# Triangular solve of a hybrid diffusion step: steps over blocks of 16 rows in place of 32, with a second level of joins on TensorE

## Chip, core and metric

The kernel runs on one core of a Trainium2 chip. The core has TensorE (PE: matrix products; PEld is its weight load), VectorE (DVE), ScalarE (ACT), GpSimd (POOL) and SyncE (SP, which issues most DMAs here). Each engine runs its own queue of instructions in order, and engines wait for one another through semaphores. PE writes to PSUM, a small memory of banks that DVE and ACT read. The metric is the device time of one execution in microseconds (us), lower is better.

## What is computed

The kernel is one inference step of two layers (an even layer with latent attention beside a gated DeltaNet, an odd layer with mLSTM, each followed by a SwiGLU FFN) for 512 latent tokens and 128 context tokens. The part that matters here is the solve in the DeltaNet of the even layer. For each chunk of 64 tokens, head and direction, a strictly lower triangular 64x64 matrix plus the identity is inverted:

```python
def gated_delta_scan(q, k, v, g, beta, s0):
    ...
    a_mat = jnp.where(strict, jnp.einsum('cbhid,cbhjd->cbhij', kb, kc) * decay, 0.0)
    t_mat = lax.linalg.triangular_solve(a_mat + eye, jnp.broadcast_to(eye, a_mat.shape),
                                        left_side=True, lower=True)
    u = jnp.einsum('cbhij,cbhjv->cbhiv', t_mat, vc * bc[..., None])
    w = jnp.einsum('cbhij,cbhjd->cbhid', t_mat, kb * jnp.exp(gc)[..., None])
    ...
    s, o = lax.scan(step, s0.astype(F32), (u, w, attn, q_dec, k_dec, g_last))
```

There are 640 tokens, so 10 chunks, 8 heads and 2 directions: 160 matrices. The scan that uses them goes from chunk to chunk in order.

## The kernel before

All tokens stand side by side (`T` = 640 columns, five tiles `t` of 128 tokens, tile 4 is the context). `even_mixer` runs in stages. It loads x, norms it and splits it into two parts `hi` and `lo`. Then it makes the columns of the combined input projection one by one: `col(u)` runs 48 matmuls of 128x320 (`lin`, L369), and a few small matmuls for the modulation of later layers go before each (`ada_step`, L498, whose weights `wa` come by SP). The columns are, in order: k and q columns (`kqv_col`), five latent columns with the five calls of `chunk(t, d_)` between them, the four v columns (`kqv_col(8)` to `(11)`) and the four z columns (`gz_col`). A v column is read by ACT into `pad`, convolved on DVE (`y`, L1041), goes through a tanh on ACT and becomes `vF` on DVE (L1050); PE transposes `vF` (L1070) in the middle of a later column. PSUM holds two wide tiles `mm` and three single ones.

`chunk(t, d_)` (L1084 and on) writes the masked matrices into `Bg[g]`: group 0 holds tiles 0 and 1, group 1 tiles 2 and 3, group 2 tile 4 (half as many). A `Bg` is [128, 32, 64]: partitions are two halves `hf` of 64 rows, then 32 matrices, then 64 columns.

`solve` inverts the 32x32 blocks on the diagonal. A 32x32 transpose on DVE (L1372, L1375) turns `Bg` so that each of the 128 partitions owns one block, whose 1024 elements lie in the free dimension (`X`, and `X2` for group 2). Then 31 steps follow, two instructions each: an outer product into `tmp` (L1386) and a subtraction from `X` (L1387). Step j works on (31-j)*(j+1) elements. Groups 0 and 1 run on DVE, group 2 on POOL. A mask `low` clears what lies above the diagonal (L1395, L1396).

`solved` joins two inverted 32x32 blocks into a 64x64 inverse, group by group: DVE transposes back (`DT` L1403, `DN` L1404), PE forms `Z` (L1412, a 32x32 matmul for each matrix and half, 64 for a full group), ACT copies it with its sign changed (L1417), PE forms the corner block (L1425 for one direction, L1427 for the other, 32 each), and ACT and POOL put the result together in `TT` (L1432 to L1441), which SP writes to `scr` in HBM. `run(solved(...), expand, 1, 1)` lets one step of `solved` alternate with one of `expand` (`mla_expand`): its q part multiplies each token tile by `w_uq` (L1560 with 384 columns), norms, transposes (L1572) and stores; its kv part (L1560 with 512 columns) follows. After `solved`, the scan (L1464 and on) reads `J` from `scr` and alternates with the rest of `expand`, then with the attention heads, and before each of these a further `ada` step is taken whose weights come through the buffers `wr`. `wa`, `wr` and `J` all go through SP's queue.

The order on each engine is not that of the source: a scheduler with a timeline of its own sorts instructions when the program is built, and an engine then keeps to that order. The lines

```python
X01, X2, low, last = solve(s, vp, Bg)
with s.tc.issue_after(last.ins):
    nc.gpsimd.tensor_tensor(rq, nqk[:, 0], v3("mhalf"), op=ALU.pow)
...
run(solved(s, s.pool("ez", 1, ez), X01, X2, low, Bg, put), expand, 1, 1)
```

are where the two functions are called.

Of the kernel before, what the change touches and what calls it, by code (L numbers as in the profile page):

```python
# [10 lines left out]
ALU = mybir.AluOpType  # L11
# [4 lines left out]
P = 128  # L16
# [20 lines left out]
TT = 3  # L37
# [8 lines left out]
def _consts():  # L46
    p = np.arange(P)
# [33 lines left out]
            ("half32", (p[:, None] // 32) % 2 == np.arange(2)[None, :]),  # L81
        ],
# [11 lines left out]
    r = {}  # L94
# [22 lines left out]
def _prep(inp):  # L117
# [4 lines left out]
    d["low32"] = np.broadcast_to(np.tril(np.ones((32, 32), f)).reshape(1, 1024), (P, 1024))  # L122
# [738 lines left out]
def even_mixer(s):  # L861
# [8 lines left out]
    with ExitStack() as es:  # L870
# [97 lines left out]
        with ExitStack() as ec:  # L968
# [226 lines left out]
            kx["p"] = s.pool("ekv", 1, ec, side="right")  # L1195
# [18 lines left out]
            X01, X2, low, last = solve(s, vp, Bg)  # L1214
# [146 lines left out]
def solve(s, pool, Bg):  # L1361


    nc = s.nc
    X = s.t(pool, [P, 2, 32, 32], "X", 1)
    X2 = s.t(pool, [P, 32, 32], "X2", 1)
    tmp = s.t(pool, [P, 3, 256], "tmp", 1)
    diag = lambda x: x.rearrange("p i c -> p (i c)")[:, 0:1024:33]
    for g, eng in ((0, nc.vector), (2, nc.gpsimd), (1, nc.vector)):
        x = X2 if g == 2 else X[:, g]  # L1370
        bv = lambda j0: Bg[g][:, :, j0:j0 + 32].rearrange("p n j -> p j n")
        nc.vector.transpose(out=x, in_=bv(0))  # L1372
        for q in (1, 3):
            r = slice(32 * q, 32 * q + 32)
            nc.vector.transpose(out=x[r], in_=bv(32)[r])  # L1375
        nc.gpsimd.memset(diag(x), 1.0)
        if g == 2:

            low = Bg[2][:, 16:, :].rearrange("p n c -> p (n c)")
            nc.sync.dma_start(low, s.I["low32"])  # L1380
            low = low.rearrange("p (i c) -> p i c", i=32)
        for j in range(31):
            n, m = 31 - j, j + 1
            sh = [P, n, m]
            tv = tmp[:, g, :n * m].rearrange("p (i c) -> p i c", i=n)
            eng.tensor_tensor(tv, x[:, j, j + 1:].unsqueeze(2).to_broadcast(sh), x[:, j, :m].unsqueeze(1).to_broadcast(sh), op=ALU.mult)  # L1386
            i = eng.tensor_tensor(x[:, j + 1:, :m], x[:, j + 1:, :m], tv, op=ALU.subtract)  # L1387
        if g == 2:
            last = i
    return X, X2, low, last  # L1390


def solved(s, pool, X, X2, low, Bg, put):
    nc = s.nc
    nc.gpsimd.tensor_tensor(X2, X2, low, op=ALU.mult)  # L1395
    nc.vector.tensor_tensor(X, X, low.unsqueeze(1).to_broadcast([P, 2, 32, 32]), op=ALU.mult)  # L1396
    Rs = [X[:, 0], X[:, 1], X2]
    for g in (0, 1, 2):
        TT = s.t(pool, [P, 32, 64], "TT", 2)

        DT = s.t(pool, [P, 32, 32], "DT", 1)
        DN = s.t(pool, [P, 32, 32], "DN", 1)
        nc.vector.transpose(out=DT.rearrange("p n i -> p i n"), in_=Rs[g])  # L1403
        nc.vector.transpose(out=DN.rearrange("p n c -> p c n"), in_=Rs[g].rearrange("p i c -> p c i"))  # L1404
        ni = 16 if g == 2 else 32
        ranges = [(0, ni // 2, 0), (ni // 2, ni, 1)]
        Zp = s.mm()
# [718 lines left out]
```

## Time and profile before

| what | us |
|---|---|
| median of 3 runs (lowest, highest) | 1851.85 (1848.32, 1854.29) |
| profiled execution: its own time | 1855.94 |
| profiled execution: span from first to last instruction | 1854.1 |

| engine, whole span | busy us | share |
|---|---|---|
| PE | 1757.3 | 95% |
| PEld | 1619.3 | 87% |
| DVE | 1192.0 | 64% |
| ACT | 744.7 | 40% |
| POOL | 465.0 | 25% |

A share is a mean over stages with different limits. Lines of the trace have the start in us from the span's start, the duration, the engine, the line of the source, the operation, out<-in with sizes, and a count where neighbours are merged; in brackets stands the idle time of that engine before it and what ended it. A plain fp32 matmul leaves two MATMUL records. PEclk is the granted clock of TensorE as a share of 2.4 GHz; the other level is 1.2 GHz.

### The profile page before, as it was taken

The numbers are of one execution on the slowest core, as the hardware profiler recorded it, in microseconds if no ns is written. First come the engines' busy times: TensorE is split into PE (matmuls) and PEld (weight loads), VectorE is DVE, ScalarE is ACT, GpSimd is POOL, SyncE is SP. The second block draws the span as 40 slices with busy tenths as digits, with TensorE's granted clock in tenths as the row PEclk, the third lists the DMA queues.
The fourth block names the chain that finished last, engine by engine and source line by source line (L and its number), as shares of the span: only waits on it lengthen the run. The fifth ranks groups of instructions, "written<-read, shape, count | busy, mean of one in ns | idle before, by whom it ended". The sixth has DMA issues, their size and how long they took to land.

```text
span 1854.1 us, 33865 instructions
## 1 busy us (share of the span) xinstructions
PE 1757.3 (95%) x13775; PEld 1619.3 (87%) x13775; DVE 1192.0 (64%) x2191; ACT 744.7 (40%) x1474; POOL 465.0 (25%) x424
## 2 busy tenths in 40 slices
PE   6998788889999989999999999999998999999999
PEld 3887678665668989999999999898998999999999
DVE  5578998665674688448637573544657873684473
ACT  3453225522345455325415343620336551453251
POOL 2024583311110154024214000021304331340230
PEclk9998888889999989999999999998999999999999
DMA  9565543696642212322322334421321233223222
GB/s 367 161 202 176 174 134 96 177 276 200 191 139 92 69 52 86 94 65 83 101 69 75 112 102 124 132 73 42 114 69 46 80 92 92 69 81 92 68 72 89
DMA packets 99327, 214.40 MB, mean 116 GB/s; under 512 B 8060, under 2 KB 44604, under 8 KB 97764
## 3 DMA queue, kind: packets, MB, share of 16 engines
q1 hardware_dynamic: 94548, 206.14, 35.9%
q10 hardware_dynamic: 4624, 6.11, 1.2%
q8 instruction: 108, 1.77, 0.4%
q14 instruction: 47, 0.39, 0.1%
HBM read 190.68 MB, written 21.54 MB: 114 GB/s over the span
## 4 chain that ended last, share of the span: by engine, by line
PE 76%; DVE 9%; DMA 6%; ACT 3%; POOL 3%; issue 2%; SPq 1%; ACTq 0%; DVEq 0%; POOLq 0%
PE mm L369 29%; PE p L350 18%; PE mm L350 12%; PE pa L498 2%; DMA wr<-in_w_ada 2%; PE p L1734 1%; PE p L1757 1%; PE p L1997 1%; PE p L1744 1%; PE p L2001 1%; SPq L1893 1%; ACT hf L787 1%; DMA D<-grd 1%; PE p L399 1%; PE p L1530 1%
## 5 line engine op out<-in xcount | busy, mean ns | idle before, releaser
L284 ACT CAST wp<-wr 128x1024 fp32r<-128x1024 f32 (+2 forms) x224 | 187.9, 839 | 502.3 <-PE mm L369 360.2
L369 PE MATMUL mm<-hi,wp 128*128 128x320 f32 x1696 | 336.3, 316 | 1.1 <-DVE x L542 0.7
L285 DVE TENSOR_TENSOR wp<-wr,wp 128x1024 fp32r<-128x1024 f32 (+2 forms) x220 | 255.9, 1165 | 75.8 <-ACT wp L284 68.6
L369 PEld LDWEIGHTS mm<-hi,wp 128*128 128x128 f32 x1696 | 271.5, 191 | 14.6 <-issue 9.9
L369 PE MATMUL mm<-hf,wp 128*128 128x320 f32 x1836 | 279.8, 311 | 0.6 <-DVE x L542 0.4
L369 PEld LDWEIGHTS mm<-hf,wp 128*128 128x128 f32 x1836 | 274.0, 189 | 1.1 <-PE mm L369 1.1
L369 PE MATMUL mm<-lo,wp 128*128 128x320 f32 x848 | 199.1, 315 | 0.2 <-DVE lo L454 0.2
L542 DVE SCALAR_TENSOR_TENSOR x<-mm,ada,x 128x320 f32<-128x320 f32 (+2 forms) x174 | 66.1, 434 | 201.5 <-PE mm L369 191.6
L350 PE MATMUL p<-T,wp 128*128 128x320 f32 x1164 | 185.4, 308 | 0.0
L350 PEld LDWEIGHTS p<-T,wp 128*128 128x128 f32 x1164 | 174.4, 188 | 0.0
L285 DVE TENSOR_TENSOR wp<-st,wp 128x512 fp32r<-128x512 f32 x160 | 137.5, 881 | 23.1 <-ACT wp L284 21.6
L369 PEld LDWEIGHTS mm<-lo,wp 128*128 128x128 f32 x848 | 144.8, 191 | 1.6 <-DVE lo L454 0.5
L350 PE MATMUL p<-B,wp 128*128 128x320 f32 x864 | 143.2, 309 | 0.0
L310 POOL TENSOR_TENSOR st<-st,wr 128x512 f32<-128x512 f32 x40 | 53.4, 1336 | 346.4 <-DMA wr<-in_w_fi 122.8
L284 ACT CAST wp<-st 128x512 fp32r<-128x512 f32 x160 | 95.9, 621 | 101.9 <-PE p L350 43.6
L350 PEld LDWEIGHTS p<-B,wp 128*128 128x128 f32 x864 | 130.9, 188 | 0.0
L350 PE MATMUL mm<-T,wp 128*128 128x320 f32 x756 | 120.0, 309 | 0.0
L350 PEld LDWEIGHTS mm<-T,wp 128*128 128x128 f32 x756 | 113.1, 188 | 0.0
L350 PE MATMUL mm<-B,wp 128*128 128x320 f32 x576 | 95.0, 309 | 0.0
L350 PEld LDWEIGHTS mm<-B,wp 128*128 128x128 f32 x576 | 87.1, 188 | 0.0
L621 POOL TENSOR_TENSOR a<-a,p 128x320 f32<-128x320 f32 x40 | 36.8, 920 | 146.0 <-DVE p L582 141.6
L310 POOL TENSOR_TENSOR st<-wr,st 128x512 f32<-128x512 f32 x40 | 69.8, 1745 | 7.6 <-DVE wp L285 7.6
(495 smaller groups left out, 2905.1 us busy)
## 6 DMA issues: line engine op xcount, KB each, us to landing
wr<-in_w_fi SPq DMA_DIRECT2D x68, 512.0 KB, 3.6
wa<-in_w_ada SPq DMA_DIRECT2D x52, 512.0 KB, 7.1
wr<-in_w_ada SPq DMA_DIRECT2D x44, 512.0 KB, 6.1
wr<-in_w_fo SPq DMA_DIRECT2D x32, 512.0 KB, 3.5
wr<-in_w_odd SPq DMA_DIRECT2D x25, 512.0 KB, 3.8
wr<-in_w_even SPq DMA_DIRECT2D x22, 512.0 KB, 4.5
J<-scr SPq DMA_DIRECT2D x20, 512.0 KB, 7.4
w<-in_w_fi SPq DMA_DIRECT2D x20, 512.0 KB, 3.6
```

Source lines behind the costliest of these rows:

```text
L284: s.nc.scalar.copy(hi, raw)
L285: (eng or s.nc.vector).tensor_tensor(lo, raw, hi.bitcast(F32), op=ALU.subtract)
L310: eng.tensor_tensor(whole[f], x, y, op=op)
L350: s.nc.tensor.matmul(out, a[:, k, :], op(k, n, p), start=(k == 0 and q == 0 and not onto), stop=(k == nk - 1 and q == 2), skip_group_check ...
L369: s.nc.tensor.matmul(ps[:, n, :320], a[:, k, :], op(k, n, p), start=(k == 0 and q == 0), stop=(k == nk - 1 and q == 2))
L399: s.nc.tensor.matmul(o, a[:, k, :], op(k, n, p), start=(k == 0 and q == 0), stop=(k == nk - 1 and q == 2))
L498: nc.tensor.matmul(ps[32 * g:32 * g + 32, :256], s.cs[:, k, :], w[:, g * 256:(g + 1) * 256], start=(k == 0), stop=(k == KD - 1))
L542: s.nc.vector.scalar_tensor_tensor(x[:, a:b], in0=ps[:, a - 320 * n:b - 320 * n], scalar=gate[:, k, i:i + 1], in1=x[:, a:b], op0=ALU.mult, ...
L621: nc.gpsimd.tensor_tensor(a1, a1, p5, op=ALU.mult)
L787: nc.scalar.activation(b_[:, r], t[:, r], AF.Identity, bias=s.sh[:, o, i:i + 1], scale=s.sw[:, o, i:i + 1])
L1530: nc.tensor.matmul(vp[hf][rows, a, b], J[rows, 0, c0:c0 + 64], vn[rows, c0:c0 + 64], start=True, stop=True)
L1734: nc.tensor.matmul(sa, qT[:, a, t, :], kf[:, a, :512], start=True, stop=True)
```

## The change

The 32x32 blocks on the diagonal are split into two 16x16 blocks. The class `Solve` takes the place of `solve` and `solved`.

- `eliminate(g)` runs for all three groups on DVE: 15 steps of two instructions, each over both 16x16 blocks at once (2*(15-j)*(j+1) elements, 1360 in the sum over j), then a mask. ACT first collects the blocks on the diagonal in `Dg` (three copies for each group), so that one DVE transpose for each group is left in place of three. ACT and POOL then clear in `Bg` all but the blocks that the new join needs.
- `joined(g, pool)` has a new first level: PE multiplies by the block below the diagonal (`Zv`), DVE forms the identity minus that (`X`, a scalar_tensor_tensor from PSUM), PE forms the 32x32 inverse (`Tv`) and its transpose (`Nv`), ACT copies both into `DT` and `DN`. That is 128 matmuls of 32x32 three times over for a full group, on all four strips of 32 partitions, and half of it for group 2. The second level is the old `solved`.
- `eliminate` of all groups and `joined` of groups 0 and 1 are called ahead of `run`, in the source behind the z columns; only `joined(2)` still alternates with `expand`.
- The pool `ekv` is closed earlier, and `Dg` gets a pool of its own.

```diff
-            kx["p"] = s.pool("ekv", 1, ec, side="right")
+            kv = ExitStack()
+            dp = s.pool("esd", 1, ec, side="right")
+            kx["p"] = s.pool("ekv", 1, kv, side="right")
...
-            X01, X2, low, last = solve(s, vp, Bg)
+            kv.close()
+            sv = Solve(s, vp, Bg, put, dp)
+            with ExitStack() as e2:
+                zp = s.pool("ez0", 1, e2, side="right")
+                for g in range(3):
+                    last = sv.eliminate(g)
+                for g in range(2):
+                    for _ in sv.joined(g, zp):
+                        pass
...
-                run(solved(s, s.pool("ez", 1, ez), X01, X2, low, Bg, put), expand, 1, 1)
+                run(sv.joined(2, s.pool("ez", 1, ez)), expand, 1, 1)
...
+    def eliminate(s, g):
...
+        nc.scalar.copy(D[:, :ni], B[:, :ni, 0:32])
+        for r in odd:
+            nc.scalar.copy(D[r, :ni], B[r, :ni, 32:64])
...
+        nc.vector.transpose(out=x, in_=D.rearrange("p n j -> p j n"))
+        nc.gpsimd.memset(s.X[:, g, 0:1024:33], 1.0)
+        nc.gpsimd.memset(x[:, 0:16, 16:32], 0.0)
+
+        h = k.c("half16")
+        for r in even:
+            nc.scalar.mul(B[r, :ni, 0:16], B[r, :ni, 0:16], h[r])
+            nc.gpsimd.memset(B[r, :ni, 16:32], 0.0)
+        nc.scalar.mul(B[:, :ni, 32:48], B[:, :ni, 32:48], h)
+        nc.gpsimd.memset(B[:, :ni, 48:64], 0.0)
...
+        for j in range(15):
+            n, m = 15 - j, j + 1
+            sh = [P, 2, n, m]
+            tv = s.tmp[:, g, :2 * n * m].rearrange("p (b i c) -> p b i c", b=2, i=n)
...
+            nc.vector.tensor_tensor(bl[:, :, j + 1:16, :m], bl[:, :, j + 1:16, :m], tv, op=ALU.subtract)
...
+    def joined(s, g, pool, bufs=1):
...
+        nc.vector.transpose(out=DT.rearrange("p n i -> p i n"), in_=X)
+        nc.vector.transpose(out=DN.rearrange("p n c -> p c n"), in_=X.rearrange("p i c -> p c i"))
         ni = 16 if g == 2 else 32
...
+        for n in range(ni):
+            for q, r in enumerate(qs):
+                nc.tensor.matmul(Zv[r, n, :], Bg[g][r, n, 32 * (q % 2):32 * (q % 2) + 32], DT[r, n, :], start=True, stop=True)
+        yield 1
+        nc.vector.scalar_tensor_tensor(X[:, :ni], in0=Zv[:, :ni], scalar=-1.0, in1=s.one.unsqueeze(1).to_broadcast([P, ni, 32]),
+                                       op0=ALU.mult, op1=ALU.add)
+        Tv, Nv = mm(), mm()
+        for n in range(ni):
+            for r in qs:
+                nc.tensor.matmul(Tv[r, n, :], DN[r, n, :], X[r, n, :], start=True, stop=True)
+        for n in range(ni):
+            for r in qs:
+                nc.tensor.matmul(Nv[r, n, :], X[r, n, :], DN[r, n, :], start=True, stop=True)
+        nc.scalar.copy(DT[:, :ni], Tv[:, :ni])
+        nc.scalar.copy(DN[:, :ni], Nv[:, :ni])
+        yield 1
```

PE behind the last z column, before (mm<-hi is that column, L435 and L436 spread the norm of the latents, L1560 is the q part of expand):

```order
L369 MATMUL mm_2493<-hi_107,wp_2332 128x320 x2
L1560 MATMUL p_2886<-wp_2422,mhi_2860 128x384
L1560 MATMUL p_2887<-wp_2422,mhi_2860 128x384
L1560 MATMUL p_3001<-wp_2422,mhi_2860 128x384
L435 MATMUL mm_2548<-th_2546,consts 128x512
L436 MATMUL mm_2548<-th_2546,consts 128x128
L1560 MATMUL p_2886<-wp_2422,mlo_2861 128x384
```

The same place now (L1435 is Z of the new level, L1442 T, L1445 N, L1455 Z of the old level, L1467 and L1469 its corner blocks; B_101, B_102 and B_103 are groups 0, 1 and 2; L1602 is expand):

```order
L371 MATMUL mm_2496<-hi_107,wp_2335 128x320 x2
L437 MATMUL mm_2551<-th_2549,consts 128x512
L438 MATMUL mm_2551<-th_2549,consts 128x128
L1435 MATMUL mm_2705<-DT_2701,B_101 32x32 x128
L1442 MATMUL mm_2835<-X_2561,DN_2702 32x32 x128
L1445 MATMUL mm_2836<-DN_2702,X_2561 32x32 x128
L1455 MATMUL mm_3095<-DT_2701,B_101 32x32 x64
L1467 MATMUL mm_3162<-X_2561,DN_2702 32x32 x32
L1435 MATMUL mm_3244<-DT_3240,B_102 32x32 x33
L1469 MATMUL mm_3162<-DN_2702,X_2561 32x32 x32
...
L1442 MATMUL mm_3941<-X_2561,DN_3810 32x32 x40
L1602 MATMUL p_3904<-wp_2425,mhi_3878 128x384
```

On PE all matmuls of groups 0 and 1, and the first of group 2, now stand between the last z column and the first matmul of expand; none of them stands among the z columns.

DVE at that place, before (L1148 norms the latents, the transposes are those of group 0, mlo is the low part that expand multiplies):

```order
L432 TENSOR_TENSOR th_2546<-consts,rs_2403 128x640
L454 TENSOR_TENSOR mlo_2861<-xx_565,mhi_2860 128x640 x3
...
L1148 SCALAR_TENSOR_TENSOR xx_565<-xx_565,params,mm_2548 128x128
L1403 STREAM_TRANSPOSE DT_2791<-X_2557 128x32x32
L1404 STREAM_TRANSPOSE DN_2792<-X_2557 128x32x32
```

And now (the two transposes of group 0, DT_2701 and DN_2702, stand 15 rows higher up; DT_3809 and DN_3810 are those of group 2, DT_3240 and DN_3241 those of group 1):

```order
L1158 SCALAR_TENSOR_TENSOR y_2545<-y_2545,mm_2496 128x640
...
L1150 SCALAR_TENSOR_TENSOR xx_565<-xx_565,params,mm_2551 128x128
L1427 STREAM_TRANSPOSE DT_3809<-X_2561 128x32x32
L1428 STREAM_TRANSPOSE DN_3810<-X_2561 128x32x32
L1437 SCALAR_TENSOR_TENSOR X_2561<-mm_2705,B_103 128x1024
L1427 STREAM_TRANSPOSE DT_3240<-X_2561 128x32x32
L1428 STREAM_TRANSPOSE DN_3241<-X_2561 128x32x32
L1437 SCALAR_TENSOR_TENSOR X_2561<-mm_3244,B_103 128x1024
L1437 SCALAR_TENSOR_TENSOR X_2561<-mm_3813,B_103 128x512
L456 TENSOR_TENSOR mlo_3879<-xx_565,mhi_3878 128x640 x3
```

On DVE the identity-minus-Z of group 0 stands behind both transposes of group 2, and the low part that expand needs stands behind that of all three groups.

## Rows read from the trace of the kernel before

**Rows 1.** Five stretches: length, busy PE, PEld, DVE, ACT, POOL, PEclk, DMA share, GB/s.
```profile
165.60:200.60 35.00, 24.07 (x208) 20.55 (x208) 34.70 (x65) 9.79 (x17) 12.79 (x11) 0.82 0.45 143
200.60:286.70 86.10, 70.97 (x456) 62.36 (x456) 85.42 (x151) 16.64 (x29) 63.92 (x70) 0.83 0.47 147
286.70:330.30 43.60, 38.67 (x727) 35.76 (x726) 35.52 (x53) 29.18 (x48) 15.10 (x13) 0.80 0.33 103
330.30:440.00 109.70, 93.84 (x1205) 65.10 (x1203) 67.61 (x186) 40.02 (x90) 23.93 (x24) 0.89 0.79 225
440.00:600.00 160.00, 156.17 (x1714) 111.76 (x1714) 97.46 (x285) 68.61 (x207) 14.35 (x24) 0.98 0.50 148
```

**Rows 2.** Timeline of PE: its waits of over 1.8 us, 165 to 289 us.
```profile
172.43 2.27 PE L421 MATMUL p<-consts,y 128*128 128x1 f32 x10 [6.84 <-DVE y L418]
...
200.58 1.08 PE L498 MATMUL pa<-wa,cond 128*32 128x256 f32 x8 [4.11 <-DMA wa<-in_w_ada]
...
230.47 1.33 PE L1070 MATMUL p<-consts,vF 128*128 128x128 f32 x5 [7.46 <-DVE vF L1050]
...
256.40 1.33 PE L1070 MATMUL p<-consts,vF 128*128 128x128 f32 x5 [5.37 <-DVE vF L1050]
...
272.98 1.69 PE L421 MATMUL p<-consts,y 128*128 128x1 f32 x10 [1.88 <-DVE y L418]
...
286.25 0.46 PE L369 MATMUL mm<-hi,wp 128*128 128x320 f32 x2
288.60 0.79 PE L1560 MATMUL p<-wp,mhi 128*128 128x384 f32 x3 [1.89 <-ACT mhi L453]
```

**Rows 3.** Line L1386, then L1387, 140 to 300 us: DVE, POOL busy.
```profile
140.00:300.00 160.00, 27.51 (x62) 19.99 (x31) 0.86 0.48 152
...
140.00:300.00 160.00, 31.93 (x62) 20.71 (x31) 0.86 0.48 152
```

**Rows 4.** Timeline of DVE: transposes and steps of the solve, and a stalled neighbour.
```profile
155.57 2.00 DVE L1372 STREAM_TRANSPOSE X<-B 128x1024 f32<-128x1024 f32 x1
...
161.59 4.09 DVE L1375 STREAM_TRANSPOSE X<-B 32x1024 f32<-32x1024 f32 x2
...
188.17 4.07 DVE L1375 STREAM_TRANSPOSE X<-B 32x1024 f32<-32x1024 f32 x2
...
227.58 3.46 DVE L1050 SCALAR_TENSOR_TENSOR vF<-th,y 128x512 f32<-128x512 f32 x2
...
272.85 0.57 DVE L1386 TENSOR_TENSOR tmp<-X 128x112 f32<-128x112 f32 x2
273.34 0.57 DVE L1387 TENSOR_TENSOR X<-X,tmp 128x112 f32<-128x112 f32 x2
```

**Rows 5.** Timeline of PE: joins at two clocks, and a wide fp32 matmul.
```profile
305.31 1.61 PE L1412 MATMUL mm<-DT,B 32*32 32x32 f32 x89
...
307.65 1.67 PE L1427 MATMUL mm<-DN,X 32*32 32x32 f32 x58 [0.72 <-ACT TT L1438]
...
185.42 1.02 PE L435 MATMUL mm<-th,consts 128*128 128x512 f32 x2
```

**Rows 6.** Timeline of DVE and ACT: what a join waits for.
```profile
292.14 1.91 DVE L1148 SCALAR_TENSOR_TENSOR xx<-xx,params,mm 128x512 f32<-128x512 f32 x4
293.97 2.07 DVE L1403 STREAM_TRANSPOSE DT<-X 128x1024 f32<-128x1024 f32 x1
...
301.10 2.06 ACT L1417 ACTIVATE X<-mm 32x1024 f32<-32x1024 f32 x2
...
304.06 0.72 ACT L1434 ACTIVATE TT<-DT,conste 128x512 f32<-128x512 f32 x1 [0.91 <-DVE redq L1603]
...
306.45 1.15 ACT L1438 COPY TT<-mm 32x512 f32<-32x512 f32 x2
```

**Rows 7.** Timeline of PE: the kv part begins, and a wait behind it.
```profile
330.33 0.50 PE L1560 MATMUL p<-wp,mhi 128*128 128x512 f32 x1
...
355.42 0.95 PE L498 MATMUL pa<-wr,cond 128*32 128x256 f32 x6 [2.20 <-DMA wr<-in_w_ada]
```

More of the change, by code (lines that the diff above doesn't have):

```diff
@@ L81, in _consts @@
             ("half32", (p[:, None] // 32) % 2 == np.arange(2)[None, :]),
+            ("half16", (p[:, None] // 16) % 2 == 1),
         ],
@@ L1358, in softplus @@
     return z.rearrange("p (d t s) -> p d t s", d=shape[1], t=shape[2]) if len(shape) == 4 else z
[L1361 to L1376, printed above, removed]
-        if g == 2:
[L1379 to L1390, printed above, removed]
@@ L1393, in solved, with __init__, x @@
[L1393 to L1404, printed above, removed]
-        ni = 16 if g == 2 else 32
+class Solve:
+    def __init__(s, k, pool, Bg, put, dpool):
+        s.k, s.dpool, s.Bg, s.put = k, dpool, Bg, put
+        s.X = k.t(pool, [P, 3, 1056], "X", 1)
+        s.tmp = k.t(pool, [P, 3, 128], "tmp", 1)
+        low = Bg[2][:, 16:32, :].rearrange("p n c -> p (n c)")[:, :288]
+        k.nc.sync.dma_start(low, k.I["low16"])
+        s.low, s.one = low[:, :256].rearrange("p (i c) -> p i c", i=16), low[:, 256:]
+    def x(s, g):
+        return s.X[:, g, :1024].rearrange("p (i c) -> p i c", i=32)
+    def eliminate(s, g):
+        k, nc, B, x = s.k, s.k.nc, s.Bg[g], s.x(g)
+        ni = 16 if g == 2 else 32
+        odd = [slice(32, 64), slice(96, 128)]
+        even = [slice(0, 32), slice(64, 96)]
+        D = k.t(s.dpool, [P, 32, 32], "Dg", 1)
+        nc.scalar.copy(D[:, :ni], B[:, :ni, 0:32])
+        for r in odd:
+            nc.scalar.copy(D[r, :ni], B[r, :ni, 32:64])
+        if g == 2:
+            nc.gpsimd.memset(D[:, ni:], 0.0)
+        nc.vector.transpose(out=x, in_=D.rearrange("p n j -> p j n"))
[7 more added lines that the diff above has]
+        nc.gpsimd.memset(B[:, :ni, 48:64], 0.0)
+        bl = s.X[:, g].rearrange("p (b r) -> p b r", b=2)[:, :, 0:512].rearrange("p b (i c) -> p b i c", c=32)
+        for j in range(15):
+            n, m = 15 - j, j + 1
+            sh = [P, 2, n, m]
+            tv = s.tmp[:, g, :2 * n * m].rearrange("p (b i c) -> p b i c", b=2, i=n)
+            nc.vector.tensor_tensor(tv, bl[:, :, j, j + 1:16].unsqueeze(3).to_broadcast(sh), bl[:, :, j, :m].unsqueeze(2).to_broadcast(sh), op=ALU.mult)
+            nc.vector.tensor_tensor(bl[:, :, j + 1:16, :m], bl[:, :, j + 1:16, :m], tv, op=ALU.subtract)
+        return nc.vector.tensor_tensor(bl[:, :, :, 0:16], bl[:, :, :, 0:16], s.low.unsqueeze(1).to_broadcast([P, 2, 16, 16]), op=ALU.mult)
+    def joined(s, g, pool, bufs=1):
+        k, nc, Bg, X = s.k, s.k.nc, s.Bg, s.x(g)
+        TT = k.t(pool, [P, 32, 64], "TT", bufs)
+        DT = k.t(pool, [P, 32, 32], "DT", 1)
+        DN = k.t(pool, [P, 32, 32], "DN", 1)
+        nc.vector.transpose(out=DT.rearrange("p n i -> p i n"), in_=X)
+        nc.vector.transpose(out=DN.rearrange("p n c -> p c n"), in_=X.rearrange("p i c -> p c i"))
+        ni = 16 if g == 2 else 32
+        qs = [slice(32 * q, 32 * q + 32) for q in range(4)]
+        mm = lambda: k.mm().rearrange("p a (n c) -> p (a n) c", c=32)
+        Zv = mm()
+        for n in range(ni):
[14 more added lines that the diff above has]
+        yield 1
@@ L1413, in solved @@
         yield 1
-        Zs = Rs[g]
         for hf in range(2):
             r1 = slice(64 * hf, 64 * hf + 32)
-            nc.scalar.mul(Zs[r1, :ni], Zv[r1, :ni], -1.0)
-        Fp = s.mm()
+            nc.scalar.mul(X[r1, :ni], Zv[r1, :ni], -1.0)
+        Fp = k.mm()
         Fv = Fp.rearrange("p a (n c) -> p (a n) c", c=32)
@@ L1424, in solved @@
                     if d == 0:
-                        nc.tensor.matmul(Fv[64 * hf:64 * hf + 32, n, :], DN[r1, n, :], Zs[r1, n, :], start=True, stop=True)
+                        nc.tensor.matmul(Fv[64 * hf:64 * hf + 32, n, :], DN[r1, n, :], X[r1, n, :], start=True, stop=True)
                     else:
-                        nc.tensor.matmul(Fv[64 * hf + 32:64 * hf + 64, n, :], Zs[r1, n, :], DN[r1, n, :], start=True, stop=True)
+                        nc.tensor.matmul(Fv[64 * hf + 32:64 * hf + 64, n, :], X[r1, n, :], DN[r1, n, :], start=True, stop=True)
             src = DT if d == 0 else DN
             for q in range(2):
-                x, h = TT[:, n0:n1, 32 * q:32 * q + 32], s.c("half32")[:, q:q + 1]
+                x, h = TT[:, n0:n1, 32 * q:32 * q + 32], k.c("half32")[:, q:q + 1]
                 if q:
```

7 lines of the change are left out of this document (4 added, 3 removed).

## The prediction, made before the changed kernel had been run

> **What bounds the kernel now.** I began with the five stretches [rows 1]: PE is busy 70.97 of 86.10 us while the last columns are made (200.6 to 286.7, "the column phase"), 38.67 of 43.60 in the q part of expand, and 156.17 of 160 from 440 on. PE is the bound in all of them, and DVE, although busy 85.42 of 86.10 in the column phase, matters only where PE waits for it. So the second view was PE's timeline with its waits [rows 2]. Between 200 and 287 PE waits 7.46, 5.37 and 1.88 us for DVE, because `vF` and `y` stand in DVE's queue behind steps of the solve. Before that there is one wait of 6.84 us for DVE's `y` and one of 4.11 us for the DMA of `wa`. From 440 on PE is full at a clock of 0.98, so what an earlier stage gains or loses is carried to the end almost whole. I sum shifts of PE's path, and check at each place whether DVE or ACT becomes later than PE.
>
> The profiled execution took 1855.94 us, 4.09 above the median of the three runs; I sum against it and take 4 off at the end.
>
> **1. Chunk stage, 165.6 to 200.6: −8.** The `y` for which PE waits 6.84 us [rows 2] stands on DVE behind three transposes of `solve`: 2.00 and two of 4.09 together [rows 4], with a first step or two about 7 us. The change leaves one transpose for each group, and the order puts the solve's work behind this `y`. The whole wait goes. The `wa` wait (4.11) ends on a DMA that SP issues behind one that waits for DVE; DVE stands there in the two transposes of 4.07 [rows 4], which go too. I take 1 of 4.11 at least and 4 at most. 6 to 11, I take 8, low in the range, since a transfer has its own time.
>
> **2. Column phase, 86.1 now: −21.** The waits of 7.46, 5.37 and 1.88 are 14.7 us [rows 2]. In addition the granted clock is 0.83 there [rows 1]: with two levels of 1.0 and 0.5 that is 34% of 86.1 = 29 us at half clock. About 15 of these are the waits themselves; the other 14 hold work that at full clock takes 7. 86.1 − 14.7 − 7 = 64, and I take 65 for what is left of waits (64 to 72, the upper end with no gain of clock).
>
> DVE must fit below that. Of its 85.42 busy [rows 1] nearly all of the solve's 27.51 and 31.93 [rows 3] lies here (52 of 59), with 5.9 of transposes and 2.3 of masks; 25 are left. Some of these 25 are stalls (`vF` at 227.58 holds DVE for 3.46 us [rows 4]), so 25 is on the high side. New: 90 instructions of 91 elements in the mean; those of 112 elements follow each other two in 0.49 (272.85 to 273.34 [rows 4]), so at most 90 × 0.245 = 22. Three transposes of 2.0 are 6, three masks 2, and the two transposes of group 0's join (L1427, L1428) 2 × 2.07 = 4.1 [rows 6]. 25 + 22 + 6 + 2 + 4 = 59, below 65: PE bounds, if narrowly. What ACT gets (nine copies, six scalings of at most 2 us, some 12 in all) goes into 16.64 busy of 86.10, and is covered; POOL loses its 19.99 + 20.71 of the solve [rows 3]. If DVE fits badly, a `vF` comes late as now, and up to 7 of the 21 are lost.
>
> With −8 the last column ends at about 286.7 − 8 − 21 = 257.7.
>
> **3. From the last column to expand's first matmul: 1.9 now [rows 2], 46.7 then: +44.8.** This is the price. In PE's new order all joins of groups 0 and 1 stand after the last z column and before the first L1602 (expand), so expand cannot cover them. Step by step, PE's record at 16 ns: L1412's 89 records take 1.61 [rows 5], less some 0.17 for the last one's drain.
> - To X of group 0: L437/L438 1.3 (L435 takes 1.02 [rows 5]), L1150 on DVE 1.9 and then both transposes of group 2, 2 × 2.07 [rows 6], before L1437; L1437 reads 1024 elements from PSUM, twice what one L1148 reads in 1.91/4 = 0.48, so 1.0 and 0.2 for semaphores. With 0.4 of other semaphores 9. Z of group 0 (256 records, 4.1) lies beside these transposes.
> - T and N: 256 matmuls, 512 records, 8.2.
> - ACT's copy of N 1.05 (half of L1417's 2.06 [rows 6]), a mask as L1434 0.72, the two copies of −Z 2.06, semaphores 0.3: 4.1.
> - Corners: 1.0, ACT's 1.15 as L1438 [rows 6] and 0.2, then 1.0: 3.3.
> - Group 1: its second transpose 2.1, L1437 1.2, 0.2: 3.5 (its Z beside), then 8.2, 4.1 and 3.3 again.
> - Group 2's first T matmuls and `mhi`: 3.
>
> 9 + 8.2 + 4.1 + 3.3 + 3.5 + 8.2 + 4.1 + 3.3 + 3 = 46.7. The disputed size is the record. L1412 works on two strips of 32 partitions; the new level uses four, which no row shows. If four overlap as two do, a record costs 16 × 2/4 = 8 ns; if PE falls to its low clock, it is the 25 ns of L1427 after its 0.72 wait (58 records in 1.67 [rows 5]). About 1024 records lie bare, so 8 ns gives −8 and 25 ns gives +9. I take 16, the row of the same form at full clock. Term 3 is 40 to 56.
>
> The rows show two strips that write one PSUM bank at 16 ns a record, where a record of 512 columns takes up to 1.02/2 = 0.51 us, that is 32 ns for 32 columns one after another [rows 5]; so two strips do overlap. The Trainium skill, "TensorEngine Tiling (Array Packing)", section "Gotcha 1: PSUM Pressure", says that different row tiles cannot access one bank at the same time; by it this change, whose four strips share a bank, would stay at the single pace, 32 ns, and term 3 would be 16 us longer. The trace does not agree for two strips; for four no row shows it.
>
> **4. q part of expand, 41.7 now (288.6 to 330.3): −10.7.** L435/L436 are no longer in it (−1.5). The join records of groups 0 and 1 leave it: about 512 at a mean of 18.5 ns, between the 16 and 25 above, −9.5. ACT's waits between them go, 2.4 of the 4.93 us that PE idles there [rows 1]. Group 2 brings about 300 records in place of 96, +3.3 at 16 ns, and a wait more or two, +1; the clock there is 0.80 and may rise a little, −1.6. 31 (27 to 34).
>
> **5. Behind it: −4.** The kv part starts at 330.33 now [rows 7]; from 330 to 440 PE idles 109.7 − 93.84 = 15.9 us [rows 1], part of it (2.20 [rows 7]) on `wr` DMAs in SP's queue. With groups 0 and 1 in `scr` before expand begins, the scan's `J` loads can go out earlier against the kv part. I take a quarter of the idle time, −4, between −8 and +3 (J loads ahead of `wr` in SP's queue).
>
> **Sum.** −8 − 21 + 44.8 − 10.7 − 4 = +1: 1857 for a profiled execution, 1853 for the median. Two large terms cancel: the columns get rid of DVE's waits, and PE pays the same time bare at their end.
>
> **Rivals.**
> - *A, as summed:* 1853, between 1846 and 1857.
> - *B, four strips overlap:* a record of the new level costs 8 ns, −8 in term 3 and −1 in term 4, and the `wa` wait goes whole with the column phase at 64, −4: about 1839. For it: two strips overlap already. Against it: one PSUM bank for all strips, and the short bursts with ACT and DVE waits between. The rows are as above; the Trainium skill, "TensorE: Matmul & The Clock Gate", section "Measured speedup vs the span model", says that tiles on different strips add some 4 ns each; at that, term 3 would be 12 shorter. No row bears it out on four strips.
> - *C, slower, the low clock in the joins:* the chain of term 3 is matmul bursts of 2 to 8 us with waits of 3 to 5 us on ACT and DVE between. After such waits the rows show 25 ns a record (L1427), and the clock of the stretch with the joins is the lowest of the five, 0.80 [rows 1]. 1024 × 9 ns = +9 in term 3, +2 in term 4, and the first matmuls of expand begin at half clock, about +3: 1867. It decides against the old kernel once a record in term 3 costs over 21 ns (with +5 it passes 1857.4). Strips that shut each other out of the bank give the same time.
> - *D, slower, the columns don't come sooner:* DVE's 59 of 65 us leave little slack, and the order inside decides; if two of the three `vF`/`y` waits stay (7.46 and 5.37) with half clock around them, 19 of the 29 us of terms 1 and 2 are lost: 1872. Against it: DVE loses 59.44 of steps [rows 3] for 22.
>
> **How the numbers follow.** What a measurement of this kernel can tell from no change is about 0.3%, 5.6 us. A 0.38, B 0.33, C 0.19, D 0.10. A's time is the forecast, 1853; its own range ends at about the same bound (1846.3 to 1857.4), so it is "within 0.3%". B is "faster", C and D are "slower" (0.29). The range takes in B and C, with the bounds of terms 1 and 2 on B's side (−5) and D's lower half: 1834 to 1872; outside lie B with every other bound low, and the worse half of D.
>
> **What the profile of the changed kernel would show.** Term 1: no wait of 6.84 at `y` L418. Term 2: last L371 matmul of the z columns at 256 to 266, DVE waits there below 3 us in sum. Term 3: first L1602 at about 304; L1442 and L1445 at 16 ns a record (B: near 8; C: 25 and PEclk near 0.5). Term 4: the first 512-column L1602 about 31 us after the first of 384. Term 5: the distance from there to the end 4 us shorter. The forecast is wrong if the joins of groups 0 and 1 are bare for under 35 us or over 60, or if DVE still holds up the columns by more than 7.

## The result, and the profile of the changed kernel

| | before | changed |
|---|---|---|
| median, us (lowest, highest) | 1851.85 (1848.32, 1857.08) | 1870.65 (1866.34, 1877.72) |
| span of the profiled execution, us | 1854.1 | 1868.9 |

The ratio is 1.0106, 95% interval 1.0073 to 1.0140: the change costs 1% of the time. The forecast was 1853 and "no difference"; the range (1834 to 1872) holds the result, on the side to which 0.29 was given.

Six stretches of the changed kernel, to be read against [rows 1]; columns as there: length, busy PE, PEld, DVE, ACT, POOL, PEclk, DMA share, GB/s.

```profile
165.60:189.30 23.70, 21.99 (x211) 18.79 (x209) 18.98 (x34) 11.88 (x17) 12.90 (x11) 1.00 0.62 196
189.30:253.40 64.10, 61.80 (x458) 54.98 (x458) 58.36 (x140) 27.74 (x47) 15.80 (x18) 1.00 0.61 190
253.40:323.00 69.60, 41.80 (x2261) 38.39 (x2260) 15.46 (x15) 18.77 (x25) 4.80 (x6) 0.55 0.15 48
323.00:356.20 33.20, 29.26 (x455) 26.26 (x451) 19.21 (x41) 18.11 (x34) 10.78 (x9) 0.86 0.36 93
356.20:440.00 83.80, 72.45 (x898) 50.96 (x900) 56.33 (x152) 30.98 (x61) 21.63 (x18) 0.92 0.88 244
440.00:600.00 160.00, 152.83 (x1809) 100.72 (x1805) 97.55 (x298) 70.03 (x221) 16.30 (x28) 0.99 0.51 150
```

The first two rows hold the same columns as 165.6 to 286.7 before: PE is busy almost without a break, at full clock. The third row is new: 69.6 us between the last column and expand's first matmul (L1602), PE busy for 41.8 of them at a clock of 0.55. The timeline of PE at its beginning and its end (start, duration, line, count, and in brackets the idle time before and what ended it):

```profile
252.93 0.46 PE L371 MATMUL mm<-hi,wp 128*128 128x320 f32 x2
...
255.87 1.69 PE L1435 MATMUL mm<-DT,B 32*32 32x32 f32 x178 [1.40 <-DVE y L1158]
261.29 1.29 PE L1435 MATMUL mm<-DT,B 32*32 32x32 f32 x78 [3.73 <-issue]
263.91 0.95 PE L1442 MATMUL mm<-X,DN 32*32 32x32 f32 x50 [1.33 <-DVE X L1437]
265.02 1.93 PE L1442 MATMUL mm<-X,DN 32*32 32x32 f32 x128 [0.16 <-issue]
268.48 1.23 PE L1442 MATMUL mm<-X,DN 32*32 32x32 f32 x76 [1.52 <-issue]
...
271.93 1.93 PE L1445 MATMUL mm<-DN,X 32*32 32x32 f32 x128 [1.52 <-issue]
275.38 1.13 PE L1445 MATMUL mm<-DN,X 32*32 32x32 f32 x69 [1.52 <-issue]
...
322.99 1.01 PE L1602 MATMUL p<-wp,mhi 128*128 128x384 f32 x2
```

Two things are to be seen. In a piece without a hole the pitch (the time from one record's start to the next) is short. It is the duration of the piece less that of a single record, over the records that are left: 178 records in 1.69 us, (1.69 - 0.17)/177 = 8.6 ns at full clock, and later 128 in 1.93, (1.93 - 0.24)/127 = 13.3 ns at the low clock. The clock is 0.96 from 256 to 261 and 0.50 from 261.3 on: it fell during the first hole. Yet PE stops in the middle of a loop whose matmuls wait for nothing: "issue" means that the profile shows no releaser. The stops come every 128 records whatever the line is, and from one to the next it is 268.48 - 265.02 = 3.46 and 271.93 - 268.48 = 3.45 us, 27 ns a record (in group 1, from 298.78 to 302.51 and 306.51, 3.73 and 4.00). The waits of the stretch by cause (total, times, longest):

```profile
PE mm L1445 <- issue: 6.9, 4, 2.1
PE mm L1435 <- issue: 5.6, 2, 3.7
PE mm L1467 <- ACT X L1459: 3.7, 4, 1.1
PE mm L1442 <- DVE X L1437: 3.6, 3, 1.4
PE mm L1442 <- issue: 3.6, 4, 1.5
PE mm L1455 <- issue: 2.2, 2, 1.2
PE mm L1435 <- DVE y L1158: 1.4, 1, 1.4
PE mm L1469 <- ACT TT L1480: 0.9, 2, 0.4
```

18.3 of the 27.8 us of idle time are "issue". The profile has DMA queues of the kind "instruction". Between 255 and 323 the busiest of them moved (queue, kind: packets, MB, share of the DMA engines):

```profile
q8 instruction: 17, 0.28, 1.7%
```

That is a packet of 16 KB every 4 us; in the old kernel the 130 us from 200 to 330 had 9. In the two holes from 268.5 to 275.4 there are 2 packets: one for each piece of 128 records and their 128 weight loads. So the first theory of the study, **S** (supply): PE's instructions arrive in pieces of 128 records and no faster than one piece in some 3.45 us; a run of small matmuls that is longer than what is on hand goes at 27 ns a record, not at its own 8.6 or 13.3. Its rivals: **K**, the low clock is the price and the holes are incidental; **P**, strips shut one another out of a PSUM bank; **W**, the waits on ACT and DVE between the levels; **M**, the matmuls are too many wherever they stand.

### The profile page after: what moved, and what is told of

Read it like the earlier page. It is cut to its first block, busy times and chain, and to the rows that moved or that the text cites. A ratio compares the mean times of both kernels' runs of the same rounds, so it can differ in the third digit from the quotient of the medians.

```text
span 1868.9 us, 37656 instructions
## 1 busy us (share of the span) xinstructions
PE 1768.6 (95%) x15695; PEld 1629.4 (87%) x15695; DVE 1146.9 (61%) x2156; ACT 764.9 (41%) x1498; POOL 424.3 (23%) x374
## 5 line engine op out<-in xcount | busy, mean ns | idle before, releaser
L371 PE MATMUL mm<-hi,wp 128*128 128x320 f32 x1696 | 330.4, 312 | 1.1 <-DVE x L544 0.7
L371 PEld LDWEIGHTS mm<-hi,wp 128*128 128x128 f32 x1696 | 266.1, 188 | 13.3 <-issue 8.5
```

What stands on the lines that cost most here:

```text
L371: s.nc.tensor.matmul(ps[:, n, :320], a[:, k, :], op(k, n, p), start=(k == 0 and q == 0), stop=(k == nk - 1 and q == 2))
```

## Experiments

Medians of the kernel before, taken beside the runs, were 1850.8 in the first group of runs (the first four), 1853.1 (the next three), 1849.4 (two) and 1854.2 (the last two).

### 1. N issued twice

```diff
+        for n in range(ni):
+            for r in qs:
+                nc.tensor.matmul(Nv[r, n, :], X[r, n, :], DN[r, n, :], start=True, stop=True)
         for n in range(ni):
             for r in qs:
                 nc.tensor.matmul(Nv[r, n, :], X[r, n, :], DN[r, n, :], start=True, stop=True)
```

> The changed kernel with the matmuls of N issued twice over: 512 more records in the bare run of joins of groups 0 and 1, no new wait on ACT or DVE. The stretch from the end of the last column to expand's first matmul is 70.2 us in the changed kernel. Theory S (supply): 512 x 27 ns = +13.8, 84 us, nearly all of it as further holes on 'issue' or stretched pieces. Theory K (low clock, 13.5 to 14 ns a record): +7, 77 us. If neither counts (8.5 ns a record, the pitch of the first piece of 178 records): +4.4, 74.6.

One time, 1895.5 us. The stretch (last column's end at 253.97, first L1605 at 339.94) is 86.0 against 69.6 us: +16.4, 32 ns for each of the 512 added records, none of which waits for another engine. S said 13.8, K 7 (the 70.2 us of the expectations is this stretch, counted from a little earlier). The pieces here are 3.45 to 4.0 us apart, 27 to 31 ns a record. The holes stand in the added loop (L1448) as in the old one:

```profile
277.17 1.23 PE L1445 MATMUL mm<-DN,X 32*32 32x32 f32 x76 [1.80 <-issue]
...
280.62 1.93 PE L1448 MATMUL mm<-DN,X 32*32 32x32 f32 x128 [1.52 <-issue]
284.08 1.13 PE L1448 MATMUL mm<-DN,X 32*32 32x32 f32 x69 [1.52 <-issue]
```

### 2. N on DVE

```diff
-        Tv, Nv = mm(), mm()
+        Tv = mm()
...
-        for n in range(ni):
-            for r in qs:
-                nc.tensor.matmul(Nv[r, n, :], X[r, n, :], DN[r, n, :], start=True, stop=True)
         nc.scalar.copy(DT[:, :ni], Tv[:, :ni])
-        nc.scalar.copy(DN[:, :ni], Nv[:, :ni])
+        nc.vector.transpose(out=DN[:, :ni], in_=DT[:, :ni])
```

> The changed kernel with N made by a 32x32 transpose of the copied T on DVE in place of PE's 128 matmuls and ACT's copy: 512 fewer records in the bare run. DVE waits there anyway, 18 and 26 us at a time. Theory S (supply): -13.8 and about -2 for ACT's copies of N that the next step waited for, the stretch falls from 70.2 to 52 to 57 us, time 1854 to 1858. Theory K: -7 and -2, 61 us, time 1860 to 1863. Theory W (waits on ACT and DVE between the levels are what costs): -2 at most, 68 us, time 1867 to 1871.

Median 1861.0, ratio to before 1.0053 (1.0030 to 1.0076). The stretch is 56.6 us (251.66 to 308.29), 13.0 shorter, 25 ns for each record left out. S had the stretch right (52 to 57, K 61, W 68). The whole time fell by 9.7, less than S's 12 to 16, and 1861.0 is a time that K gave: the kv part starts 16.1 us earlier than in the changed kernel (340.13, 356.18), but the first matmul of the output projection comes 242.7 us behind that, 239.8 in the changed kernel, and a few us more are lost behind the projection, where the kernels are alike. The transpose of DVE is short:

```profile
269.59 1.25 DVE L1444 STREAM_TRANSPOSE DN<-DT 128x1024 f32<-128x1024 f32 x1 [7.00 <-ACT DT L1443]
```

### 3. Two banks in turn

```diff
-            for r in qs:
-                nc.tensor.matmul(Tv[r, n, :], DN[r, n, :], X[r, n, :], start=True, stop=True)
+            for q, r in enumerate(qs):
+                m = (n + ni // 2 * (q % 2)) % ni
+                nc.tensor.matmul(Tv[r, m, :], DN[r, m, :], X[r, m, :], start=True, stop=True)
```

The same for Z and N.

> The changed kernel with the order of the new level's matmuls changed so that neighbours on PE write to two PSUM banks in turn (strips 0 and 2 work half a group ahead of strips 1 and 3); the same count, the same result. Theory P (strips shut one another out of a bank): the pitch of a piece without holes falls below 8.5 ns and the stretch of 70.2 us shrinks by 5 us or more. Theories S, K and W: within 2 us of 70.2, the same pitch and the same holes.

One time, 1868.3 us; the stretch is 69.9 us (253.61 to 323.52), and the first piece reads as before:

```profile
256.09 1.69 PE L1436 MATMUL mm<-DT,B 32*32 32x32 f32 x178 [1.41 <-DVE y L1158]
261.57 1.28 PE L1436 MATMUL mm<-DT,B 32*32 32x32 f32 x78 [3.79 <-issue]
```

178 records in 1.69 us with one bank or with two: P falls. As the prediction read the rule of the Trainium skill ("TensorEngine Tiling (Array Packing)", section "Gotcha 1: PSUM Pressure"), strips that share a bank would have shown a longer pitch than strips that don't; the trace does not agree, for four strips of 32x32 fp32, each of which writes 32 partitions of its own.

### 4. Joins beside expand

```diff
-                for g in range(2):
-                    for _ in sv.joined(g, zp):
-                        pass
...
-                run(sv.joined(2, s.pool("ez", 1, ez)), expand, 1, 1)
+                zp = s.pool("ez", 1, ez)
+                run((x for g in range(3) for x in sv.joined(g, zp)), expand, 1, 1)
```

> The joins of all three groups alternate with expand, as the joins of the kernel before do; the steps over 16 rows and the new level are kept. Theory S (PE's instructions arrive too slowly for a long run of small matmuls: in the changed kernel the run of joins between the last column and expand is cut by holes of 1.2 to 3.7 us that end on 'issue', about 3.45 us from one piece of 128 records to the next, 27 ns a record): wide matmuls between the joins give the supply time, so no hole on 'issue' above 0.5 us is left in the joins, the last column still ends at 252 to 256, and the kv part starts at 311 to 323 (356 in the changed kernel, 330 in the kernel before). Some of the 11 us that the changed kernel gains behind the kv part's start is lost again. Time 1836 to 1850. Theory K (the low clock in the run of joins, 0.56, is what costs): the same direction, since the clock rises beside wide matmuls, but the holes on 'issue' stay: 1845 to 1858. Theory M (the matmuls are simply too many, wherever they stand: 42 us of busy PE): the kv part starts at about 339, time 1856 to 1864.

Median 1871.5, ratio 1.0101 (1.0073 to 1.0129): no gain at all, a miss of S as I had put it. The kv part did start early (328.43, 356.18 in the changed kernel), but the joins went on until 375.6 and the holes stayed, 22.5 us of them:

```profile
274.57 2.34 PE L1440 MATMUL mm<-X,DN 32*32 32x32 f32 x254
278.88 0.20 PE L1440 MATMUL mm<-X,DN 32*32 32x32 f32 x1 [1.98 <-issue]
...
282.34 1.93 PE L1443 MATMUL mm<-DN,X 32*32 32x32 f32 x128 [1.52 <-issue]
```

The joins of groups 0 and 1 still stand in runs of 256 to 640 records. By S, wide matmuls ahead of such a run help only by what they let be fetched in advance; here the first holes come after 151 records of Z and 254 of T. So S was put anew: not the neighbourhood but the length of a run decides. The next two runs test this form of S.

### 5. Both, and both in finer grains

The coarse kernel has the edits of 2 and 4. The fine-grained one has them too, and lets the joins give way to expand after every 32 matmuls, and expand give way inside a token tile:

```diff
         for n in range(ni):
             for r in qs:
                 nc.tensor.matmul(Tv[r, n, :], DN[r, n, :], X[r, n, :], start=True, stop=True)
+            if n % 8 == 7 and n < ni - 1:
+                yield 1
...
-        ps = tokmm(hi, lo, t, ws, 3, 384)
+        ps = yield from tokmm(hi, lo, t, ws, 3, 384)
```

Z and the old level get such yields too, and `tokmm` one after each of its `k` but the last.

> Both earlier edits together: the joins of all groups alternate with expand (as in the run with joins beside expand, 1871.5), and N is a transpose on DVE (640 records fewer on PE). In that run the pieces of joins are still 256 to 512 records long and hold 22.5 us of holes on 'issue', so standing beside wide matmuls did not help by itself. Theory S (supply of PE's instructions, 27 ns a record once a piece is longer than the 150 to 180 records that are on hand): -640 x 27 ns = -17, about 1854, holes of 6 to 12 us in all. Theory K (low clock, 13.5 ns a record): -9, 1863, holes unchanged per record.

> As the run before it, with the same instructions, but in finer grains: the joins give way to expand after every 32 matmuls (64 records) and expand gives way inside a token tile, so that most pieces of joins are 32 to 64 matmuls long between wide ones (the first two pieces stay at 128). Theory S: pieces shorter than what is on hand have no holes; 2 to 5 us of holes are left, all in the two long pieces; time 5 to 10 us below the run before, 1844 to 1850. Theory K: the count and the clock are the same, within 3 us of the run before. Theory M (the matmuls are too many in any place): within 3 us of the run before.

The coarse one: one time, 1857.6, 13.9 below the kernel of section 4 for 640 records fewer, 22 ns each (S 27, K 13.5); holes 12.1 us. The fine-grained one: median 1847.1, ratio to before **0.9970 (0.9947 to 0.9992)**, 0.3% faster than the kernel before. PE has 15055 records in both runs. The fine-grained one reads:

```profile
264.82 1.09 PE L1433 MATMUL mm<-DT,B 32*32 32x32 f32 x105 [2.04 <-issue]
...
276.25 0.22 PE L1441 MATMUL mm<-X,DN 32*32 32x32 f32 x2 [1.97 <-issue]
...
303.56 0.62 PE L1603 MATMUL p<-wp,mhi 128*128 128x512 f32 x2
304.02 0.60 PE L1617 MATMUL p<-consts,qkt 128*96 128x128 f32 x4
304.55 0.75 PE L1441 MATMUL mm<-X,DN 32*32 32x32 f32 x64
305.23 0.64 PE L1617 MATMUL p<-consts,qkt 128*96 128x128 f32 x4
305.80 0.75 PE L1441 MATMUL mm<-X,DN 32*32 32x32 f32 x64
306.48 0.73 PE L1603 MATMUL p<-wp,mhi 128*128 128x512 f32 x2
```

A piece of 64 records takes 0.75 us, (0.75 - 0.17)/63 = 9.2 ns each, with no hole. The only holes of any size, 2.04 and 1.97 us, stand in two pieces that the scheduler left at 256 records; in all 4.8 us.

How much of the 10.5 us between the two runs is due to the grain? 4.5 us are there before any join: the last column ends at 250.4 and 254.9, in code that the finer grain does not touch. From there to the output projection the fine-grained run takes 319.4 us and the coarse one 325.4: 6.0 less, for 7.3 us less of holes. So S holds in its second form, and M falls: the matmuls are the same and only their grain moved the time. K can't be told from S by this pair, since the granted clock rose too, from 0.80 (254.9 to 380) to 0.90 (250.4 to 380). K falls by sections 1 and 2, where a record cost 32 and 25 ns and K gives 13.5.

### 6. Group 0 among the z columns, and expand ahead

Two ways to cut the holes that are left. One puts the joins of group 0 between the last z columns:

```diff
+            def js(g):
+                yield from sv.joined(g, zp)
+            jj = js(0)
             for u in range(1, 4):
                 last = gz_col(u)
...
+                for _ in range(3):
+                    next(jj, None)
```

(the elimination of all groups moves ahead of the loop). The other gives expand six steps ahead of the fine-grained run:

```diff
+                for _ in range(6):
+                    next(expand)
                 run((x for g in range(3) for x in sv.joined(g, zp)), expand, 1, 1)
```

> As the fine-grained run, but the joins of group 0 really stand among the last two z columns (in pieces of 32 to 74 matmuls), those of groups 1 and 2 beside expand. Theory S: the columns end 6 to 9 us later (768 records at 8.5 ns and a wait or two), expand is 10 to 12 us shorter, next to no holes: 2 to 6 us below the fine-grained run, 1839 to 1847, faster than the kernel before. Against it (theory W): the transposes of group 0 come late on DVE and PE waits for them among the columns: 1850 or more.

> The fine-grained run (N on DVE, joins beside expand in pieces of 32 matmuls) with expand six steps ahead, so that the two pieces of 128 matmuls, which hold 4.0 us of its holes on 'issue', are cut to 8 to 64 as well. Nothing else changes, but the joins end some 5 us later, and the scan, which needs those of groups 0 and 1, begins as much later. Theory S: no hole on 'issue' above 0.5 us is left, 3 to 5 us below the fine-grained run, 1842 to 1845. Theory L (the scan's late beginning is what bounds by now): the holes go, but waits behind 340 take their place, 1846 to 1851.

Group 0 among the columns: median 1859.8, ratio 1.0035 (1.0018 to 1.0052). That is W's side (1850 or more): the columns end at 265.8, and PE waits among them and behind them (230 to 300):

```profile
PE mm L1441 <- DVE DT L1433: 5.3, 2, 3.3
PE mm L1474 <- ACT X L1466: 1.8, 2, 1.1
PE mm L1449 <- DVE X L1444: 1.5, 1, 1.5
```

Not all of it is W: from 300 to 600 PE waits 22.7 us for `wr`, 13.5 in the fine-grained run.

The second: median 1860.0, ratio 1.0044 (1.0027 to 1.0061). The holes in the joins are gone but for one of 1.2 us, and still the time is 13 us above the fine-grained run, beyond what either theory said. One wait of 4.2 us without a releaser now stands elsewhere, amid the modulation's matmuls, which are no long run of small ones; what it is stays open:

```profile
345.04 2.34 PE L500 MATMUL pa<-wr,cond 128*32 128x256 f32 x17 [4.21 <-issue]
```

The last column ends 3.6 us later than in the fine-grained run (253.9, 250.4), the scan begins at 374.5 in place of 365.3, and the output projection, which needs it, at 581.5 in place of 569.8. From the scan's first matmul to the projection's it is 204.0 us in section 4, 205.4 in the coarse run, 204.5 in the fine-grained one, 206.9 here. In these four runs the scan begins 58 to 75 us behind the kv part, and it looks as if it then set the end; that is argued from the four distances and not tested.

### 7. An earlier scan

The fine-grained run with two pieces of joins for each step of expand, and with three pieces of half the size:

```diff
-                run((x for g in range(3) for x in sv.joined(g, zp)), expand, 1, 1)
+                run((x for g in range(3) for x in sv.joined(g, zp)), expand, 2, 1)
```

> The fine-grained run (N on DVE, joins beside expand in pieces) with two pieces of joins for each step of expand in place of one. Pieces get longer, so some more holes on 'issue' come back (8 to 14 us in place of 4.8), but the joins end sooner and with them the scan's beginning: from its first matmul to the first matmul of the output projection it takes 204 to 207 us in the four runs in which it begins at 365 to 392, and 230 to 244 in those in which it begins at 338 to 355. Theory L (a scan that begins after about 350 is the bound): it begins at 330 to 345 now, the output projection at 552 to 564 (569.8 in the fine-grained run), time 1828 to 1841. If supply alone counts (theory S without L): more holes, so 3 to 8 us above the fine-grained run, 1850 to 1855.

> Between the two runs: pieces of 16 matmuls, three for each step of expand. The scan begins some 5 us later than with two pieces of 32, with fewer holes. Theory L: 1830 to 1843, within 4 us of the run with two pieces of 32. Theory S without L: 1848 to 1853.

Medians 1863.2, ratio 1.0064 (1.0042 to 1.0085), and 1862.2, 1.0054 (1.0033 to 1.0074): slower than either theory said. The scans did begin earlier (342.1 and 353.1), and yet the projection came later, at 587.1 and 583.3, 245.0 and 230.2 us behind. Theory L's threshold does not hold either: with N issued twice the scan begins at 375.5 and the projection 244.1 us behind it, and in the run of section 8 at 362.1 and 235.1 behind. What the four runs near 205 us share is that the kv part had started long before the scan, not the time at which the scan begins. PE's first cause of waits from 250 to 600 in the fine-grained run, and then in the run with two pieces:

```profile
PE pa L500 <- DMA wr<-in_w_ada: 13.5, 7, 4.0
```

```profile
PE pa L500 <- DMA wr<-in_w_ada: 23.0, 14, 4.9
PE mm L1466 <- ACT X L1458: 5.4, 4, 3.6
PE mm L1441 <- issue: 4.9, 2, 2.5
PE mm L1433 <- issue: 4.2, 2, 2.2
```

Holes of 9.1 against 4.8 us, 9.5 us more for the `wr` of the modulation steps, and 5.4 us for ACT. The run with half-size pieces, for which fewer holes had been expected, has 11.7 us of them and 21.1 us for `wr`. What sets the best place of the scan between these ends is left open; loads of `J` and `wr` in one queue are a likely reason, and were not tried apart.

### 8. Group 2's steps on POOL

```diff
+            e = nc.gpsimd if g == 2 else nc.vector
...
-            nc.vector.tensor_tensor(bl[:, :, j + 1:16, :m], bl[:, :, j + 1:16, :m], tv, op=ALU.subtract)
+            e.tensor_tensor(bl[:, :, j + 1:16, :m], bl[:, :, j + 1:16, :m], tv, op=ALU.subtract)
```

The outer product likewise.

> The changed kernel with the 15 steps of group 2 on POOL, as the 31 steps of group 2 were in the kernel before; everything else as in the changed kernel. It takes 30 steps of about 0.25 us off DVE. Theory D1 (the columns came sooner because DVE has fewer elements to go through): the last column ends within 1.5 us of the changed kernel's 253.2, or a little sooner, since DVE gets freer. Theory D2 (a good part came from DVE no longer sharing with POOL): DVE's steps and y beside POOL's steps get longer, 0.3 to 0.5 us in place of 0.2 to 0.25, PE waits again for vF or y, and the last column ends 3 us or more later. Time 1867 to 1872 by D1, 1872 to 1878 by D2.

One time, 1871.8. The last column ends at 260.8 in place of 253.4; 3.1 us of that are there before the steps begin (L437 of the earlier norm at 181.30 in place of 178.24), so 4.3 are the edit's: the column phase (from the first L500 behind `asb` to the end of the last column) takes 68.4 us, and 62.0 to 64.7 in the ten runs that keep group 2's steps on DVE and all joins behind the columns. DVE's steps beside POOL got longer, in the mean (180 to 255; busy, mean ns):

```profile
L1419 DVE TENSOR_TENSOR X<-X,tmp 128x30 f32<-128x30 f32 (+7 forms) x30 | 10.3, 361 | 0.2
L1418 DVE TENSOR_TENSOR tmp<-X 128x30 f32<-128x30 f32 (+7 forms) x30 | 9.8, 343 | 0.5 <-POOL X L1403 0.3
L1418 POOL TENSOR_TENSOR tmp<-X 128x30 f32<-128x30 f32 (+7 forms) x15 | 8.0, 533 | 0.9
```

The subtraction takes 361 ns against 323 in the changed kernel, the outer product 343 against 330, and PE waited 5.1 us for `vF` in place of 1.8. That is D2's sign, in one run; the time of the whole doesn't tell D1 from D2.

## Why the prediction was right or wrong, step by step

| term | predicted | measured | from |
|---|---|---|---|
| 1 chunk stage | -8 | -11.3 | first L498/L500 after `asb`: 200.58, now 189.30 |
| 2 column phase | -21 | -22.0 | 86.1, now 64.1 |
| 3 bare joins | +44.8 | +67.7 | 1.9, now 69.6 |
| 4 q part of expand | -10.7 | -8.5 | 41.7, now 33.2 |
| 5 behind it | -4 | -11.1 | 1523.8, now 1512.7 |
| sum of the profiled spans | +1 | +14.8 | 1854.1, now 1868.9 |

**Terms 1 and 2 were right, mechanism and size.** The waits of [rows 2] are gone (0.60 us at `y`, in sum 2.3 at `vF` and `y` among the columns), the clock went from 0.83 to 1.00, and the column phase took 64.1 us where 65 was taken. DVE was busy for 58.4, as the 59 of the check. Term 1 came out at the upper end that the text gave (11), since the 4.11 us for `wa` went as a whole.

**Term 3 is the step that failed.** Its order was right: the joins of groups 0 and 1 stand bare, and the steps came in the order written down. Its size was not: they are bare for 69.6 us, beyond the 60 that the prediction itself named as its sign of being wrong. "PE's record at 16 ns" was taken from L1412, in pieces of at most 128 records [rows 5], and no run of joins in the kernel before is longer than some 160. With four strips a record costs 8.6 ns (rival B was right on that), and at the low clock 13.3 (rival C was right that the clock falls: 0.55). But a run of 512 records goes at neither price: it took 12.6 and 13.0 us, some 25 ns a record, near the 27 ns at which its pieces of 128 come. Along the chain, where 9, 8.2, 4.1, 3.3, 3.5, 8.2, 4.1, 3.3 and 3 had been written, PE took 10.5, 12.6, 6.0, 6.0, 6.1, 13.0, 5.8, 6.0 and 3.6. Of the 22.9 us that the term lacked, 9.2 are the long runs of T and N. 4.1 are the two steps that end on the new level's Z: it was to lie beside DVE's transposes, but with its holes (3.7 and 1.8 us) it ended after them, and DVE waited 1.5 and 2.5 us for it. 3.6 are the steps with the old level's Z, which have a hole each (1.2 and 1.0), 0.6 the last step. The 5.4 of the corners have no hole: they run at the low clock, 58 records in 1.76 us, and wait for ACT. So 16.9 of the 22.9 us stand in steps with holes; the 18.3 us of holes are not to be taken off one for one, since the records of T and N between them go faster than the 16 ns of the sum.

**Term 4** was 2 us too hopeful: PE waits 3.28 us for ACT (`st`) at 349.05.

**Term 5** has two parts. From the kv part's start to the output projection 3.7 us were gained (243.5, now 239.8), as the -4 said; whether by earlier `J` loads, as it took, is not shown. The other 7.3 lie behind the projection, where the kernels are alike. In the third 320 us after it the old kernel's profiled execution had a lower clock than the new one's, and got through 40 records less, some 6 us of work (windows of before, then of after; the same columns as above):

```profile
1213.82:1533.82 320.00, 310.90 (x2098) 293.65 (x2097) 208.31 (x390) 127.05 (x231) 88.98 (x79) 0.96 0.23 74
```

```profile
1235.95:1555.95 320.00, 310.35 (x2138) 293.82 (x2137) 211.79 (x392) 128.02 (x232) 88.51 (x80) 0.99 0.23 74
```

The code of this stretch is the same, so I put this down to the two executions and not to the change. The profiled execution of before was 4.1 us above its median, and the medians differ by 18.8, the spans by 14.8.

**The rivals.** B's pitch came true and its result did not (its terms add up to 1840, not 1839); C's low clock came true, at 13.3 ns in place of 25; D did not happen. D's time, 1872, lay nearest to the result and C's, 1867, next, and neither for the reason that it gives: that the range held is luck. A fifth case was missing, and it decided: that PE could be short of instructions.

## What to carry to other kernels

When a change adds many small matmuls, price them twice: by the pitch of a short piece, and by the longest run in which they will stand, since a run longer than any in the old trace can meet a limit that no row shows. Cutting the runs into pieces between wide matmuls and taking a third of the new level off PE (a DVE transpose of 1.25 us in place of 128 matmuls) turned +1.0% into -0.3%, with the steps over 16 rows kept. And of the 30 us by which the kv part starts earlier in that run than in the kernel before (299.9, 330.3), 4 were left at the output projection (569.8, 573.8): follow a gain to the next consumer before counting it.

## What the runs showed of the hardware

- Where nothing wide stood between, PE went through long runs of small fp32 matmuls at one piece of 128 records (with their weight loads) in 3.45 to 4.0 us, with one 16 KB packet of the instruction queue a piece; a first run of 151 to 254 records went through without a hole. The records added in section 1 cost 32 ns each, those taken away in section 2 saved 25. That the packets are what PE waited for is argued from their pace; what sets that pace no run shows.
- Four strips of 32x32 fp32 matmuls take 8.6 to 9.2 ns a record at full clock and 13.3 at the low one; two strips 16 at full clock. Alternating between two banks made no difference. The Trainium skill ("TensorE: Matmul & The Clock Gate", section "Measured speedup vs the span model") gives some 4 ns for each further tile; the traces agree that strips overlap, at about twice that figure for a record, of which an fp32 matmul leaves two.
- A 32x32 transpose on DVE whose two sides are both contiguous took 1.25 us for 1024 elements a partition (section 2); those with a strided side took 1.90 to 2.10 in the changed kernel.
